# Opening with four heads' keys in float32 by k and a fixed order; block products with B22 in buffers of its own and T3 by accumulating transfers

## The chip, the cores and the metric

The kernel runs on one core of one Trainium2 chip. The metric is the device time of one execution in microseconds; the median of several runs counts. Engines are named as in the profile: PE is TensorE (matrix products, with PEld its weight loads), DVE is VectorE, ACT is ScalarE, POOL is GpSimd and SP is the sync engine, which here only issues transfers.

## The reference, cut to what matters

One decoder layer over x (512 tokens, 1024 channels) with a memory mem (256 rows of 1024). h = RMSNorm(x) is projected into five branches (a convolution module, stick-breaking attention, an mLSTM, a gated linear recurrence, attention over the memory); each branch is gated, projected up to 1024 channels, weighted with a sigmoid gate and summed. The sum goes through one output projection, x is added, and a last RMSNorm follows. All inputs and outputs are float32.

```python
y_m = memory_attention(m_q, rmsnorm(mem, mem_norm_g), w_mkv) * silu(m_z)   # keys and values: mem_n @ w_mkv
...
for n, y in enumerate((y_a, y_b, y_c, y_d, y_m)):
    merged = merged + gates[:, :, n] * (y @ w_up[n])
x = x + merged @ w_out
return rmsnorm(x, final_norm_g)
```

## The kernel before, in words

**Numbers.** Nearly every float32 product is made of three single-pass products: each operand is split into a rounded high part (`hi`, one copy on ACT) and a rest (`lo`, one subtraction on DVE), and hi*hi + hi*lo + lo*hi are accumulated. Products of plain float32 operands are also possible; each of them shows as two records in the trace. A second way to make `lo` is used where DVE is the busier engine: ACT writes -f, rounded, into lo, and a transfer issued from POOL adds f to it in place (`accum_op=ALU.add`).

**Program order and queues.** The program is written with a planner that orders the instructions of each engine by a simulated timeline and puts in the semaphores. Instructions of one engine run in the order that the planner gave them, and so do the transfers of one issuing engine. `tc.high_priority` moves instructions forward in that plan, `tc.issue_after(ins)` keeps what is inside behind `ins` on the same engine, and `behind(ends)` does so for several. Pools have a fixed number of buffers under each tag; a tile waits until a buffer of its tag is released.

**Weights.** `load_w` (line 161) brings a 512 KB block into one of two staging buffers (`wst`) through SP's queue and splits it in two halves into the tags `whi` and `wlo` (six buffers each). The staging buffer comes free when both halves are split, and only then can the next block but one be issued. `queued` holds the last such transfer.

**Opening** (lines 250 to 375). Ten small products warm TensorE up. Then come:

- the memory's keys, `keys(h)`: for heads 0 and 1 float32 products of the weights `wkf[h]` with the scaled, transposed memory `mt` (8 steps of 128 channels, `k`); for heads 2 and 3 split operands (`memH`, `memL`, and weights through `load_w`), head after head;
- the memory's values, `values(u, w)`: four blocks of two k each, 12 products of 512 columns a block (two row halves, three products, two k);
- x: four tiles of 128 tokens are loaded, squared and summed on ACT, scaled on DVE by the root of the mean (`rx`, line 342), transposed on TensorE (`x_T(k)`, four 128x128 transposes for one of three `pj` banks), and evicted into `hH` (ACT) and `hL` (DVE);
- the row sums of mem, two transposes of their roots (`rps`), and the scaling of keys and values.

The order in which TensorE takes the values and the transposes is left to the planner.

**Middle.** `STEPS` and `ENDS` list, by hand, the order of projections, heads, gates (`G`) and up-projections (`U`).

**End** (lines 1100 to 1300). The output projection is done as seven block products over a 2x2 division (512-row halves of the weights by 512-column halves), from sums and differences of blocks. The weights' blocks and their combinations are called b11, b21, n4, T1, T2, T3 and b22; `operand` (line 1077) splits such a block into `woH` and `woL` (six buffers of each). `product` issues the products for two row tiles into two PSUM banks (`X`, `Z`, `W`, `Y`, `L`), `take` adds a bank to the residual rows `xr` on DVE, and `finish` squares a finished piece on ACT (`junk`, with the sum in `ss`), collects the sums (`v`), prepares `quarter`, multiplies the row with the norm's weights (line 1207), and for the last piece of a row tile takes the root (`root`, ACT), forms 1/root with one Newton step (DVE), scales both halves and issues the two stores. Some banks are used twice without clearing: the second product into X, the one with T3, may begin only when `take` has read what the first left there, and likewise the last product, with b22, on Y.

T3's blocks load through `block` into the staging tag `wst`, are subtracted in place (`minus`), and are split with ACT and DVE. b22 loads into the same two staging buffers, after them, and is split with accumulating transfers. `s2_end` and `s4_end` are the last splits of two sums of the left operand.

Of the kernel before, what the change touches and what calls it, by code (L numbers as in the profile page):

```python
# [80 lines left out]
def build(ctx, tc, x, mem, memT, cols_d, rows_d, wcm, wbv, wcv0, wcv1, wmk, wmv, wup, wout, dw, fg, out):  # L81
# [78 lines left out]

    def load_w(src, n, scale=None, stage=wpool):

        st = stage.tile([P, 1056], F32, tag="wst", name="wst", bufs=WST)
        queued[0] = nc.sync.dma_start(out=st[:, :n], in_=src)
        res = []
        m = n // 2
        for half in range(2):
            hi = wpool.tile([P, 576], F32R, tag="whi", name="whi", bufs=WHL)
            lo = wpool.tile([P, 576], F32R, tag="wlo", name="wlo", bufs=WHL)
            f = st[:, half * m:(half + 1) * m]  # L170
            with tc.high_priority(offset=PREP):
                if scale is None:
                    act(hi[:, :m], f, AF.Copy)  # L173
                    V.tensor_tensor(out=lo[:, :m], in0=f, in1=f32(hi[:, :m]), op=ALU.subtract)  # L174
# [85 lines left out]
    wkf = [spool.tile([P, D], F32, name=f"wkf{h}") for h in range(2)]  # L260
# [30 lines left out]
    def keys(h, w=None):  # L291

        ps = kps[h // 2][:, (h % 2) * NMEM:(h % 2 + 1) * NMEM]
        for k in range(NK):
            go, end = h % 2 == 0 and k == 0, k == NK - 1
            if w is None:
                mm(ps, lhsT=wkf[h][:, k * P:(k + 1) * P], rhs=mt[:, k, :], start=go, stop=end, skip_group_check=True)  # L297
            else:
                mm3(ps, [(*piece(w, k, P, 4), memH[:, k, :], memL[:, k, :])], first=go, last=end, check=True)

    keys(0)
    keys(1)
# [4 lines left out]
    wk = [load_w(wmk[h], D, stage=spool) for h in (2, 3)]  # L307
    keys(2, wk[0])
    keys(3, wk[1])
# [8 lines left out]
    def values(u, w):  # L318
        for kk in range(2):
            k = 2 * u + kk  # L320
            wh, wl = piece(w, kk, 512, 1)
            for m in range(2):
                sl = slice(m * P, (m + 1) * P)
                mm(vps[m], lhsT=memH[:, k, sl], rhs=wh, start=k == 0, stop=False)
                mm(vps[m], lhsT=memH[:, k, sl], rhs=wl, start=False, stop=False)
                mm(vps[m], lhsT=memL[:, k, sl], rhs=wh, start=False, stop=k == NK - 1)

    def x_T(k):
        tp = pj.tile([P, S], F32, tag="pj", name="tp")
        for i in range(NT):  # L330
            nc.tensor.transpose(tp[:, i * P:(i + 1) * P], xt[i][:, k * P:(k + 1) * P], ident)
        act(hH[:, k, :], tp, AF.Copy, scale=col("norm_g", k))
        V.scalar_tensor_tensor(out=hL[:, k, :], in0=tp, scalar=col("norm_g", k), in1=f32(hH[:, k, :]),
                               op0=ALU.mult, op1=ALU.subtract)

    values(0, wv[0])
    values(1, wv[1])
# [5 lines left out]
    for k in range(4):  # L343
        x_T(k)
    values(2, load_w(wmv[2], D))
    for k in range(4, NK):
        x_T(k)
    values(3, load_w(wmv[3], D))
# [7 lines left out]
    for m in range(2):  # L356
        nc.tensor.transpose(rps[:, m * P:(m + 1) * P], rc[:, m:m + 1].broadcast_to([P, P]), ident)
# [719 lines left out]
    def operand(f, add=False):  # L1077
# [3 lines left out]
        if add:  # L1081
            act(lo, f, AF.Copy, scale=-1.0)
            G.dma_start(out=lo, in_=f, accum_op=ALU.add)
            act(hi, f, AF.Copy)
        else:
            split_sb(f, hi, lo)
# [96 lines left out]
    def finish(t, half, cs=slice(0, S)):  # L1183
# [15 lines left out]
        if end:  # L1199
            V.tensor_scalar(v, ss, sums[t], 0.25, op0=ALU.add, op1=ALU.mult)  # L1200
        else:
            V.tensor_scalar_add(v, ss, sums.get(t, EPS))
        sums[t] = v
        if n == pieces[t] - 1:
            quarter[t] = epool.tile([P, 1], F32, name=f"quarter{t}")
            V.tensor_scalar_mul(quarter[t], v, 0.25)
        V.tensor_tensor(out=xo, in0=xo, in1=rows[:, cs], op=ALU.mult)
        if not end:
            return
# [34 lines left out]
    with behind(s4_end):  # L1244
        b22 = [operand(block(1, 1, u), True) for u in range(2)]
# [20 lines left out]
def _layout(a):  # L1266
# [25 lines left out]
    wmk = wm[:, :, :E].reshape(NK, P, 4, P).transpose(2, 1, 0, 3).reshape(4, P, NK * P)  # L1292
# [30 lines left out]
```

## Time and profile before

| | us |
|---|---|
| median of 3 runs | 840.95 (840.57 to 841.35) |
| the profiled execution | 839.85 |
| its span | 838.1 |
| PE busy | 821.7 |
| DVE, ACT busy | 599.2, 499.4 |
| DMA, mean | 131 GB/s |

The profile is of one execution. Its span runs from the first to the last recorded instruction; 1.75 us of its time lie around the span. A row of the timeline gives the start, the duration from there to the end of the last of its instructions, engine, line, operation, out<-in, shape and count, and in square brackets how long the engine had been idle before it and what ended that wait. Rows with a count of several are merged neighbours. Matmuls overlap, so the distance between starts is the cost of one, not the duration in its row.

### The profile page before, as it was taken

How to read it: one execution, taken by the hardware profiler on the slowest of the kernel's cores; microseconds unless marked ns; L12 is line 12 of the kernel's file. 1: busy time of each engine (PE TensorE's matmuls, PEld its weight loads, DVE VectorE, ACT ScalarE, POOL GpSimd, SP SyncE). 2: the span in 40 equal slices, each digit the busy share in tenths (PEclk: the TensorE clock that was granted, in tenths of full speed). 3: DMA queues.
4: the chain of work that ended last, by engine and by line, in shares of the span. 5: the costliest groups of instructions: out<-in, count | busy, mean ns of one | idle time of the engine just before them, and what ended most of it. 6: DMA issues, size and time to landing. Idle time of an engine off the chain costs nothing.

```text
span 838.1 us, 11376 instructions
## 1 busy us (share of the span) xinstructions
PE 821.7 (98%) x4028; PEld 693.8 (83%) x4028; DVE 599.2 (71%) x1139; ACT 499.4 (60%) x895; POOL 105.2 (13%) x157
## 2 busy tenths in 40 slices
PE   8999999999999999999999999999999999999995
PEld 7788888888898889788888988888888888888874
DVE  4879989997456677785675767559667575458976
ACT  6644475635545554667556546585465977954564
POOL 0000020101100222022333000010100200200020
PEclk9999999999999999999999999999999999999998
DMA  9432274445624334436625243563352745675184
GB/s 356 155 128 98 89 152 112 105 123 134 156 88 126 90 88 101 119 88 144 152 77 121 80 142 98 145 157 101 108 132 75 154 119 147 138 254 195 37 212 128
DMA packets 36848, 109.47 MB, mean 131 GB/s; under 512 B 4148, under 2 KB 4276, under 8 KB 36792
## 3 DMA queue, kind: packets, MB, share of 16 engines
q1 hardware_dynamic: 24376, 84.11, 30.7%
q0 software_dynamic: 11552, 23.07, 16.3%
q10 hardware_dynamic: 864, 1.57, 0.5%
q8 instruction: 31, 0.51, 0.2%
q14 instruction: 25, 0.20, 0.1%
HBM read 103.49 MB, written 2.11 MB: 126 GB/s over the span
## 4 chain that ended last, share of the span: by engine, by line
PE 89%; DVE 6%; DMA 2%; ACT 2%; issue 1%; ACTq 0%; SPq 0%; DVEq 0%
PE pj L212 24%; PE pj L211 24%; PE pj L210 24%; PE pj L541 2%; PE pj L539 2%; PE pj L540 2%; PE po L653 1%; PE wb L639 1%; DMA wst<-in 1%; PE og L844 1%; PE mk L297 1%; DVE wlo L174 1%; PE zb L610 1%; PE zb L609 1%; DMA mt<-in 1%; DVE woL L229 1%
## 5 line engine op out<-in xcount | busy, mean ns | idle before, releaser
L212 PE MATMUL pj<-hH,wlo 128*128 128x512 f32 x768 | 300.0, 391 | 0.3 <-DVE wlo L174 0.3
L211 PE MATMUL pj<-hL,whi 128*128 128x512 f32 x768 | 299.7, 390 | 0.0
L210 PE MATMUL pj<-hH,whi 128*128 128x512 f32 x768 | 299.5, 390 | 0.0
L173 ACT ACTIVATE whi<-wst 128x512 fp32r<-128x512 f32 (+1 forms) x180 | 111.6, 630 | 161.6 <-PE pj L211 116.9
L174 DVE TENSOR_TENSOR wlo<-wst,whi 128x512 fp32r<-128x512 f32 (+1 forms) x180 | 122.2, 686 | 75.5 <-ACT whi L173 75.1
L212 PEld LDWEIGHTS pj<-hH,wlo 128*128 128x128 f32 x768 | 144.2, 188 | 30.3 <-DVE wlo L174 0.7
L211 PEld LDWEIGHTS pj<-hL,whi 128*128 128x128 f32 x768 | 144.3, 188 | 29.7
L210 PEld LDWEIGHTS pj<-hH,whi 128*128 128x128 f32 x768 | 144.3, 188 | 29.2
L194 POOL DMA_DIRECT2D wlo<-in x72 | 62.7, 871 | 531.8 <-ACT wlo L193 394.8
L427 DVE SCALAR_TENSOR_TENSOR acc<-u,cols,acc 128x512 f32<-128x512 f32 x120 | 88.6, 746 | 1.4
L195 ACT ACTIVATE whi<-wst 128x512 fp32r<-128x512 f32 x72 | 45.3, 630 | 55.6 <-PE pj L211 40.0
L211 PE MATMUL pj<-yL,whi 128*128 128x512 f32 x160 | 62.5, 390 | 0.0
L210 PE MATMUL pj<-yH,whi 128*128 128x512 f32 x160 | 62.4, 391 | 0.0
L212 PE MATMUL pj<-yH,wlo 128*128 128x512 f32 x160 | 62.3, 390 | 0.0
L193 ACT ACTIVATE wlo<-wst 128x512 fp32r<-128x512 f32 x72 | 44.5, 618 | 5.9 <-PE at L540 4.0
L212 PEld LDWEIGHTS pj<-yH,wlo 128*128 128x128 f32 x160 | 30.0, 188 | 6.2
L210 PEld LDWEIGHTS pj<-yH,whi 128*128 128x128 f32 x160 | 30.0, 188 | 6.1
L211 PEld LDWEIGHTS pj<-yL,whi 128*128 128x128 f32 x160 | 30.1, 188 | 5.9
L629 DVE TENSOR_TENSOR_SCAN kp<-kp 128x512 f32<-128x512 f32 (+3 forms) x32 | 26.8, 858 | 10.9 <-POOL kp L622 10.6
L540 PE MATMUL pj<-wlo,hH 128*128 128x256 f32 (+1 forms) x112 | 31.8, 284 | 0.0
L541 PE MATMUL pj<-whi,hL 128*128 128x256 f32 (+1 forms) x112 | 31.8, 284 | 0.0
L539 PE MATMUL pj<-whi,hH 128*128 128x256 f32 (+1 forms) x112 | 31.5, 283 | 0.0
(395 smaller groups left out, 1262.3 us busy)
## 6 DMA issues: line engine op xcount, KB each, us to landing
wst<-in SPq DMA_DIRECT2D x132, 512.0 KB, 3.3
wlo<-in POOLq DMA_DIRECT2D x72, 256.0 KB, 5.2
xt<-in SPq DMA_DIRECT2D x4, 512.0 KB, 9.4
raw<-in SPq DMA_DIRECT2D x4, 512.0 KB, 6.6
t<-in SPq DMA_DIRECT2D x4, 512.0 KB, 5.2
woL<-t POOLq DMA_DIRECT2D x4, 512.0 KB, 6.4
wst<-in SPq DMA_DIRECT2D x2, 528.0 KB, 4.3
mr<-in SPq DMA_DIRECT2D x2, 512.0 KB, 10.6
```

The costliest lines, as they stand in the source:

```text
L173: act(hi[:, :m], f, AF.Copy)
L174: V.tensor_tensor(out=lo[:, :m], in0=f, in1=f32(hi[:, :m]), op=ALU.subtract)
L193: act(lo[:, :m], st[:, sl], AF.Copy, scale=-1.0)
L194: G.dma_start(out=lo[:, :m], in_=src[:, sl], accum_op=ALU.add)
L195: act(hi[:, :m], st[:, sl], AF.Copy)
L210: mm(ps, lhsT=ah, rhs=bh, start=first and i == 0, stop=False, skip_group_check=check)
L211: mm(ps, lhsT=ah, rhs=bl, start=False, stop=False, skip_group_check=check)
L212: end = mm(ps, lhsT=al, rhs=bh, start=False, stop=last and i == n - 1, skip_group_check=check)
L427: V.scalar_tensor_tensor(out=a, in0=u[:, k:k + S], scalar=col("a_w", i * 31 + k), in1=a, op0=ALU.mult, op1=ALU.add)
L539: mm(dst[t], lhsT=hH[:, k, tsl], rhs=wh, start=first, stop=False, skip_group_check=True)
L540: mm(dst[t], lhsT=hH[:, k, tsl], rhs=wl, start=False, stop=False, skip_group_check=True)
L541: mm(dst[t], lhsT=hL[:, k, tsl], rhs=wh, start=False, stop=k == NK - 1, skip_group_check=True)
```

## The change

In the opening all four heads' keys are float32 products. Their weights come in a layout by k (`wkf`, 128 x 8 x 512), in pieces of one, one, two, two and two k, over ACT's queue (the first three) and SP's, with mt in four pieces of one, one, two and four k. The products run k by k with the heads inside; no key weight is split any more. TensorE's order of values, transposes and the two `rps` transposes is written out (`in_order`), and each eviction of a transpose is queued behind the last value split so far (`prep`), so that the third and the fourth value block are split earlier than the planner put them.

At the end, the T3 blocks are split with accumulating transfers, and b22 is loaded in four halves into four `wlo` buffers right after the last projections' weights, ahead of T3's loads in SP's queue, and split by halves from there. The table of functions that holds the root is loaded behind the last s4 split. In `finish`, the row multiplication of a piece that is not the last comes behind `v` and `quarter`.

```diff
-    wkf = [spool.tile([P, D], F32, name=f"wkf{h}") for h in range(2)]
+    wkf = spool.tile([P, NK, 4 * P], F32, name="wkf")
...
-    for i in range(2):
-        sl = slice(i * 512, i * 512 + 512)
-        nc.scalar.dma_start(out=wkf[0][:, sl], in_=wmk[0][:, sl])
-    nc.scalar.preload_act_table_set("sqrt_and_others")
-    for c in ((0, 2), (2, 4), (4, 8)):
-        nc.sync.dma_start(out=mt[:, c[0]:c[1], :], in_=memT[:, c[0]:c[1], :])
-    nc.sync.dma_start(out=wkf[1], in_=wmk[1])
+    for i, c in enumerate((slice(0, 1), slice(1, 2), slice(2, 4), slice(4, 8))):
+        nc.sync.dma_start(out=mt[:, c, :], in_=memT[:, c, :])
+        if i < 3:
+            nc.scalar.dma_start(out=wkf[:, c, :], in_=wmk[:, c, :])
+        if i == 1:
+            nc.scalar.preload_act_table_set("sqrt_and_others")
+    for c in (slice(4, 6), slice(6, 8)):
+        nc.sync.dma_start(out=wkf[:, c, :], in_=wmk[:, c, :])
...
-    keys(0)
-    keys(1)
+    for k in range(NK):
+        for h in range(4):
+            end = mm(kps[h // 2][:, (h % 2) * NMEM:(h % 2 + 1) * NMEM], lhsT=wkf[:, k, h * P:(h + 1) * P],
+                     rhs=mt[:, k, :], start=h % 2 == 0 and k == 0, stop=k == NK - 1, skip_group_check=True)
...
-    wk = [load_w(wmk[h], D, stage=spool) for h in (2, 3)]
-    keys(2, wk[0])
-    keys(3, wk[1])
...
+    last_pe = [end]
+    def in_order(f):
+        with tc.issue_after(last_pe[0].ins):
+            last_pe[0] = f()
...
+        with behind(prep):
+            act(hH[:, k, :], tp, AF.Copy, scale=col("norm_g", k))
+            V.scalar_tensor_tensor(out=hL[:, k, :], in0=tp, scalar=col("norm_g", k), in1=f32(hH[:, k, :]),
+                                   op0=ALU.mult, op1=ALU.subtract)
...
+    wv.append(load_w(wmv[2], D))
+    prep = prepared[0]
+    for u, kk in ((0, 0), (0, 1), (1, 0)):
+        values(u, kk, wv[u])
...
+    values(1, 1, wv[1])
+    x_T(0)
+    x_T(1)
+    values(2, 0, wv[2])
+    wv.append(load_w(wmv[3], D))
+    prep = prepared[0]
+    x_T(2)
+    x_T(3)
+    values(2, 1, wv[2])
+    x_T(4)
+    x_T(5)
+    values(3, 0, wv[3])
+    x_T(6)
+    x_T(7)
+    values(3, 1, wv[3])
...
         if add:
-            act(lo, f, AF.Copy, scale=-1.0)
-            G.dma_start(out=lo, in_=f, accum_op=ALU.add)
-            act(hi, f, AF.Copy)
+            parts = f if isinstance(f, list) else [f]
+            w = D // len(parts)
+            for i, p in enumerate(parts):
+                sl = slice(i * w, (i + 1) * w)
+                act(lo[:, sl], p, AF.Copy, scale=-1.0)
+                G.dma_start(out=lo[:, sl], in_=p, accum_op=ALU.add)
+            for i, p in enumerate(parts):
+                act(hi[:, i * w:(i + 1) * w], p, AF.Copy)
...
+    b22_raw = []
+    for u in range(2):
+        halves = []
+        for c in range(2):
+            f = f32(wpool.tile([P, 576], F32R, tag="wlo", name="wlo", bufs=WHL))[:, :S]
+            with tc.issue_after(queued[0].ins):
+                queued[0] = nc.sync.dma_start(out=f, in_=wout[1, 2 + u, :, c * S:(c + 1) * S])
+            halves.append(f)
+        b22_raw.append(halves)
...
         if end:
             V.tensor_scalar(v, ss, sums[t], 0.25, op0=ALU.add, op1=ALU.mult)
+            V.tensor_tensor(out=xo, in0=xo, in1=rows[:, cs], op=ALU.mult)
         else:
-            V.tensor_scalar_add(v, ss, sums.get(t, EPS))
+            prior = V.tensor_scalar_add(v, ss, sums.get(t, EPS))
...
-            V.tensor_scalar_mul(quarter[t], v, 0.25)
-        V.tensor_tensor(out=xo, in0=xo, in1=rows[:, cs], op=ALU.mult)
+            prior = V.tensor_scalar_mul(quarter[t], v, 0.25)
         if not end:
+            with behind((prior,)):
+                V.tensor_tensor(out=xo, in0=xo, in1=rows[:, cs], op=ALU.mult)
             return
...
-            T3.append(operand(minus(f, t2[u], f)))
+            T3.append(operand(minus(f, t2[u], f), True))
...
     with behind(s4_end):
-        b22 = [operand(block(1, 1, u), True) for u in range(2)]
+        nc.scalar.preload_act_table_set("sqrt_and_others")
+        b22 = [operand(f, True) for f in b22_raw]
```

More of the change, by code (lines that the diff above doesn't have):

```diff
@@ L159, in build @@
     t1, t2, n4 = [], [], []
+    prepared = [None]
     def load_w(src, n, scale=None, stage=wpool):
@@ L172, in load_w @@
                 if scale is None:
-                    act(hi[:, :m], f, AF.Copy)
-                    V.tensor_tensor(out=lo[:, :m], in0=f, in1=f32(hi[:, :m]), op=ALU.subtract)
+                    prepared[0] = (act(hi[:, :m], f, AF.Copy),
+                                   V.tensor_tensor(out=lo[:, :m], in0=f, in1=f32(hi[:, :m]), op=ALU.subtract))
                 else:
@@ L289, in build @@
     vps = [at.tile([P, S], F32, tag="at", name="mv") for _ in range(2)]
[L291 to L299, printed above, removed]
-    keys(0)
-    keys(1)
+    for k in range(NK):
+        for h in range(4):
+            end = mm(kps[h // 2][:, (h % 2) * NMEM:(h % 2 + 1) * NMEM], lhsT=wkf[:, k, h * P:(h + 1) * P],
+                     rhs=mt[:, k, :], start=h % 2 == 0 and k == 0, stop=k == NK - 1, skip_group_check=True)
     for c in range(4):
@@ L316, in build, with values, go @@
     mr = [load_row(mem, i, "mr") for i in range(2)]
[L318 to L321, printed above, removed]
+    last_pe = [end]
+    def in_order(f):
+        with tc.issue_after(last_pe[0].ins):
+            last_pe[0] = f()
+    def values(u, kk, w):
+        k = 2 * u + kk
+        wh, wl = piece(w, kk, 512, 1)
+        def go():
             for m in range(2):
@@ L325, in values, with go @@
                 mm(vps[m], lhsT=memH[:, k, sl], rhs=wl, start=False, stop=False)
-                mm(vps[m], lhsT=memL[:, k, sl], rhs=wh, start=False, stop=k == NK - 1)
+                end = mm(vps[m], lhsT=memL[:, k, sl], rhs=wh, start=False, stop=k == NK - 1)
+            return end
+        in_order(go)
     def x_T(k):
         tp = pj.tile([P, S], F32, tag="pj", name="tp")
[L330 to L337, printed above, removed]
+        def go():
+            for i in range(NT):
+                end = nc.tensor.transpose(tp[:, i * P:(i + 1) * P], xt[i][:, k * P:(k + 1) * P], ident)
+            return end
+        in_order(go)
+        with behind(prep):
[6 more added lines that the diff above has]
+        values(u, kk, wv[u])
     for i, t in enumerate(xt):
@@ L342, in build @@
         V.tensor_scalar_mul(t, t, rx[:, i:i + 1])
[L343 to L348, printed above, removed]
+    values(1, 1, wv[1])
[13 more added lines that the diff above has]
+    values(3, 1, wv[3])
     nc.sync.dma_start(out=rows, in_=rows_d.broadcast_to([P, NROW]))
@@ L356, in build @@
     for m in range(2):
-        nc.tensor.transpose(rps[:, m * P:(m + 1) * P], rc[:, m:m + 1].broadcast_to([P, P]), ident)
+        in_order(lambda: nc.tensor.transpose(rps[:, m * P:(m + 1) * P], rc[:, m:m + 1].broadcast_to([P, P]), ident))
     rm = spool.tile([P, NMEM], F32, name="rm")
@@ L1291, in _layout @@
     wm = a["w_mkv"][0].reshape(NK, P, 2 * E)
-    wmk = wm[:, :, :E].reshape(NK, P, 4, P).transpose(2, 1, 0, 3).reshape(4, P, NK * P)
+    wmk = wm[:, :, :E].transpose(1, 0, 2)
     wmv = wm[:, :, E:].reshape(4, 2, P, E).transpose(0, 2, 1, 3).reshape(4, P, 2 * E)
```

## The prediction

> **What bounds the kernel now.** I read the page first, then the busy times by stretch, then the timeline of the opening and of the end, engine by engine, and last the rows of the accumulating transfers.
>
> ```profile
> span 838.1 us, 11376 instructions
> PE 821.7 (98%) x4028; PEld 693.8 (83%) x4028; DVE 599.2 (71%) x1139; ACT 499.4 (60%) x895; POOL 105.2 (13%) x157
> ```
>
> TensorE idles 838.1 - 821.7 = 16.4 us in all. The rows below place about 12 of these at the two ends, so a change there can only win by fewer or denser products in the opening, by shorter waits in the last products, or by a shorter stretch after the last product. The middle has nothing to give. The opening:
>
> ```profile
> 6.57:14.90 8.33, 7.35 (x32) 5.78 (x33) 5.51 (x11) 6.80 (x13) 0.00 (x0) 1.00 1.03 419
> 20.85:26.32 5.47, 5.47 (x27) 4.46 (x26) 4.59 (x12) 2.74 (x6) 0.00 (x0) 1.00 0.78 304
> ...
> 1.43 4.64 PE L252 MATMUL warm<-ident 128*128 128x128 f32 x20 [1.43 <-POOL ident masks.py:199]
> 6.57 1.13 PE L297 MATMUL mk<-mt,wkf 128*128 128x256 f32 x4 [0.51 <-DVE mt L285]
> 8.49 1.13 PE L297 MATMUL mk<-mt,wkf 128*128 128x256 f32 x4 [0.78 <-DVE mt L285]
> 9.81 5.45 PE L297 MATMUL mk<-mt,wkf 128*128 128x256 f32 x24 [0.19 <-ACT mt L287]
> 14.90 0.47 PE L210 MATMUL mk<-memH,whi 128*128 128x256 f32 x1
> ...
> 26.32 1.47 PE L331 MATMUL tp<-ident,xt 128*128 128x128 f32 x12
> ...
> 29.13 1.32 PE L331 MATMUL tp<-ident,xt 128*128 128x128 f32 x8 [1.13 <-DVE hL L333]
> ...
> 37.00 0.47 PE L210 MATMUL pj<-hH,whi 128*128 128x512 f32 x1
> ...
> 37.96 0.50 PE L212 MATMUL pj<-hH,wlo 128*128 128x512 f32 x1 [0.25 <-DVE wlo L174]
> ```
>
> The two window rows give length, busy time of PE, PEld, DVE, ACT and POOL, clock, DMA share and GB/s. The keys start at 6.57, half a microsecond after the warm-up products, wait 0.78 and 0.19 for scaled pieces of mt, and end at 20.85 where the values begin. The projections start at 37.00 and stumble once (0.25 for wlo). Clock 1.00 throughout.
>
> **The keys.** Heads 0 and 1 are 16 float32 products that show as 32 records; the run of 24 lasts from 9.81 to 14.90, 0.212 us each, so 0.424 a product. Heads 2 and 3 are 48 single-pass products from 14.90 to 20.85, 0.124 each, 0.372 for three. Turning them into float32 adds 16 x (0.424 - 0.372) = 0.8 us of TensorE: alone, a loss. Against it stands the order by k. A k needs 128 KB of mt and 256 KB of weights for 4 x 0.424 = 1.7 us of products, 0.23 MB per us, while the window row shows 419 GB/s arriving, so past the first two pieces TensorE should not starve.
>
> ```profile
> 6.17 0.61 DVE L285 TENSOR_SCALAR mt<-mt,cols 128x256 f32<-128x256 f32 x2 [1.76 <-DMA mt<-in]
> ...
> 11.90 2.17 ACT L173 ACTIVATE whi<-wst 128x512 fp32r<-128x512 f32 x4
> ...
> 12.72 2.49 DVE L174 TENSOR_TENSOR wlo<-wst,whi 128x512 fp32r<-128x512 f32 x4
> ...
> 21.98 2.73 DVE L342 TENSOR_SCALAR xt<-xt,rsq_t 128x1024 f32<-128x1024 f32 x4
> ...
> 29.33 1.16 ACT L173 ACTIVATE whi<-wst 128x512 fp32r<-128x512 f32 x2
> ...
> 31.62 2.85 SPq L164 DMA_DIRECT2D wst<-in  x2
> ```
>
> The first mt piece (256 KB) is there at 6.17; half the size should be there earlier, but the warm-up holds TensorE to 1.43 + 4.64 = 6.07. I take a start at 6.1 and 32 x 0.424 = 13.6 us: the keys end at 19.7 instead of 20.85. The four whi and four wlo splits of the third and fourth head (2.17 on ACT, 2.49 on DVE) go; both engines wait for data around there, so I count nothing for that. The bytes ahead of x are the same, so x arrives as before.
>
> **The fixed order.** From 20.85 on TensorE has 48 value products at 5.47 / 24 = 0.228 (10.9 us) and 34 transposes at 1.47 / 12 = 0.12 (4.1). After: 6.1 + 13.6 + 10.9 + 4.1 = 34.7, against 37.00 plus some 0.6 for the first products (three took 37.00 to 38.29 where two steps later it is 0.23 each): effectively 37.6. A dense opening is worth 2.9. What was late before is the split of the third value block, at 29.33, although ACT was busy for only 2.74 of the 5.47 us before 26.32; it holds a staging buffer, so the weights of the first projections were issued only around 31.62. The order now queues the evictions of the transposes behind that split, which pulls the issue forward by some 4 us, and the projections can start on time. What can be late next: x is scaled by 21.98 + 2.73 = 24.7 at the earliest; the four value steps ahead of the first transpose end at 19.7 + 4 x 6 x 0.228 = 25.2. The margin is 0.5, and new splits compete for DVE there. I take 0.5 of stall: -2.4. Ends: -2.9, and +0.8 if the dearer keys buy nothing.
>
> **The end.** Times are those of the profile before.
>
> ```profile
> 798.99 2.35 DVE L1090 TENSOR_TENSOR wst<-t,wst 128x1024 f32<-128x1024 f32 x2
> ...
> 809.12 0.67 DVE L1179 TENSOR_TENSOR xr0L<-xr0L,pj 128x512 f32<-128x512 f32 x1
> ...
> 818.74 0.15 DVE L1202 TENSOR_SCALAR v<-ss 128x1 f32<-128x1 f32 x1 [4.44 <-ACT junk L1193]
> ...
> L229 DVE TENSOR_TENSOR woL<-wst,woH x2: 1208/1210/1212, 805.5 to 806.7; 128x1024 fp32r<-128x1024 f32 x2
> ...
> 800.30 2.20 ACT L229 ACTIVATE woH<-wst 128x1024 fp32r<-128x1024 f32 x2
> ...
> 816.09 1.06 ACT L1082 ACTIVATE woL<-wst 128x1024 fp32r<-128x1024 f32 x1 [2.03 <-DMA wst<-in]
> ...
> 809.94 0.47 PE L210 MATMUL pj<-woH,s2H 128*128 128x512 f32 x1 [1.79 <-DVE xr0L L1179]
> ...
> 822.56 0.47 PE L210 MATMUL pj<-woH,s4H 128*128 128x512 f32 x1 [1.18 <-DVE merged L1179]
> ...
> 828.73 0.28 PE L212 MATMUL at<-woH,s4L 128*128 128x128 f32 x1
> ```
>
> *T3 by accumulating transfers.* Before the T3 product TensorE waits 1.79 us for the eviction of X, which DVE issues at 809.12 behind the two splits woL<-wst, 2 x 1.21 = 2.4 us. They leave DVE, so the eviction comes near 806.7, before the 809.94 - 1.79 = 808.15 at which TensorE wants the bank: the wait goes. In their place come two ACT copies, two transfers on POOL's queue, and their landing. T3's blocks are formed by 798.99 + 2.35 = 801.3, the first half of that by 800.2; ACT is free at 800.30, so the two POOL issues are near 801.4 and 803.4, and T1's two and B22's four queue behind them.
>
> ```profile
> L1083 POOL DMA_DIRECT2D woL<-t x2: 867/869/871, 793.6 to 795.2; - x2
> DMA to landing us min/median/max: 6.0/6.4/6.8
> ...
> DMA to landing us min/median/max: 4.5/4.8/9.3
> ...
> 791.40:796.90 5.50, 5.50 (x26) 4.51 (x24) 5.43 (x12) 5.50 (x9) 1.74 (x2) 1.00 0.38 72
> 796.90:802.40 5.50, 5.50 (x25) 4.51 (x24) 5.50 (x11) 4.86 (x10) 2.20 (x4) 1.00 0.95 216
> ```
>
> The first landing row is T2's pair, issued at 793.6 and 795.2, so landed at about 799.6 and 802.0, 2.4 apart; the second is T1's and B22's four. With 4.5 to 6.4 the first half of T3 lands at 806 to 808, the second, 2.4 later, at 808.5 to 810; they are wanted at about 808.2 and 809.6 (six products on). I take 0.3 of new wait: -1.5. Ends: -1.8, and with 9.3 for the second (812.7, 3.1 late) +1.3.
>
> By the Trainium skill (SBUF — State Buffer, the section on two separate sides) a transfer issued from POOL can be starved of its descriptors while DVE holds the port pair they share; by that rule each of the eight issues could come one DVE operation, some 0.6 us, late, and the sum would be lighter by about 0.6. Here the two POOL issues beside a DVE that was busy 5.43 of 5.50 us took 0.87 each, as the later ones did, so this trace does not bear it out.
>
> *B22 in buffers of its own.* Before, B22 loads into the staging buffers of T3, and ACT waits for it 2.03 us ahead of 816.09, with the squares of the third row block queued behind. DVE waits 4.44 us for those squares until 818.74, and the eviction of Y behind that costs TensorE 1.18 at 822.56. In the change the four half loads take low-half weight buffers as the last projections free them, ahead of the output products, and T3's own loads queue behind them on SP: these blocks are not used until 798.99, so that costs nothing. ACT no longer waits: -1.2, ends -1.2 and 0. POOL's four issues of half the size cost 4 x 0.87 where nobody waits for POOL. Without the two stalls B22 is wanted 3 us sooner, at 819.6 and 821.0; eight transfers 2.4 apart per 512 KB from 806.6 bring its last quarter at 806.6 + 5 x 2.4 = 818.6. It fits by two microseconds.
>
> *After the last product.*
>
> ```profile
> 823.25 1.28 ACT L1196 ACT_TABLE_LOAD   x1
> 824.54 0.29 ACT L1196 ACTIVATE root<-ss,quarter 128x1 f32<-128x1 f32 x1
> ...
> 832.28 0.15 DVE L1206 TENSOR_SCALAR quarter<-v 128x1 f32<-128x1 f32 x1
> ...
> 832.74 0.29 ACT L1196 ACTIVATE root<-ss,quarter 128x1 f32<-128x1 f32 x1 [0.44 <-DVE quarter L1206]
> ...
> 834.47 0.34 ACTq L1219 DMA_DIRECT2D out<-xr1L  x1
> ```
>
> The last product ends at 829.0, the last result leaves at 834.47. In between DVE works off a backlog that began at 823.25, where a table load holds the first root and DVE waits behind it. The load moves to about 800, where ACT pays the same 1.28; quarter, held until 832.28 by the row multiplication, comes directly behind v. Undelayed, the way is eviction 0.3, square 0.5, root 0.3, reciprocals 0.6, scaling 0.7, with 0.2 of handovers 2.6, against 834.47 - 829.01 = 5.5: 2.8 at best. Finishing four row blocks keeps DVE occupied, so I take -2.0; ends -2.8 and 0.
>
> The Trainium skill (ScalarE: Activation LUTs, what a table load costs) puts a switch at some 2.7 us with its drain; by that, moving it would be worth 1.4 more, and the sum 8.5. In the trace the root starts at 824.54, 0.01 after the load ends, so 1.28 is the price here.
>
> **Sum.** -2.4 - 1.5 - 1.2 - 2.0 = -7.1. The profiled execution took 839.85 us (838.1 and 1.75 around it), so 832.75; the median of the runs, 840.95, lies 1.1 above it: 833.8. From no change a measurement tells about 0.2%, 1.7 us.
>
> **Rivals.**
> - *The opening gives little.* The order is rigid: if scaling of x or a value split comes 2 us late, TensorE waits where it used to choose another product. For: margin 0.5 at 25.2. Against: DVE has 2.5 us less to do. Then -0.3 instead of -2.4: 835.9.
> - *The end gives little.* T3 lands 3.1 late and B22 follows: T3 +1.3, Y and end -1.5 together, opening -2.4: 838.3. For: the 9.3 row; DMA share 0.95 between 796.9 and 802.4. Against: that 9.3 lay beside B22's plain loads, which move away.
> - *Slower.* The accumulating transfers run one behind the other at s per 512 KB. B22's last quarter lands at 806.6 + 5s and is wanted at 821.0, so it delays above s = 2.9 and eats the whole sum at s = (7.1 + 14.4) / 5 = 4.3. At 4.5, the shortest single landing, it is 8.1 late: 842. Against: T2's pair landed 2.4 apart.
> - *No effect.* The planner reorders the middle and new waits there give the gain back: 840. TensorE has no idle there that shows such sensitivity.
>
> **How the numbers follow.** Forecast 0.62, opening 0.16, end 0.10, slower 0.05, no effect 0.07. The forecast's own range, from its ends, is 831 to 835.6; taking in the first two rivals gives 830.8 to 838.3, with some 0.15 outside. Faster 0.87, same 0.07, slower 0.06.
>
> **What would show it.** Right: first key product near 6.1, 64 float32 key records without a gap, first projection product by 35.2, at most 0.5 of wait at the T3 product and none at the last, no table load after the last product's start, last output issued within 4 us of the last product. Wrong: waits of products on hL, wlo or xt before 35; TensorE waiting for woL in T3 or B22; DVE idle on ACT near the evictions; idle TensorE between 40 and 780.

## The result, and the profile after

The changed kernel takes 834.44 us in the median of four runs (834.15 to 834.65), the kernel before 840.76 in four (839.69 to 841.35): a ratio of 0.9929 (95% interval 0.9917 to 0.9941). The forecast was 833.8 with a range of 830.8 to 838.3. The profiled execution of the changed kernel took 834.15 us with a span of 832.1; before it was 839.85 and 838.1. So the span lost 6.0 us, where the prediction had summed 7.1. The head of the page:

```profile
span 832.1 us, 11361 instructions
PE 821.4 (99%) x4012; PEld 694.0 (83%) x4012; DVE 595.1 (72%) x1133; ACT 499.5 (60%) x897; POOL 108.8 (13%) x161
```

TensorE is as busy as before (821.4 against 821.7), so nearly all of the gain is idle time: 832.1 - 821.4 = 10.7 us instead of 16.4. The opening in the timeline of TensorE, then two rows of DVE and one of ACT (the split of the third value block, which was at 29.33 before):

```profile
5.51 1.99 PE L296 MATMUL mk<-mt,wkf 128*128 128x256 f32 x8
8.97 12.35 PE L296 MATMUL mk<-mt,wkf 128*128 128x256 f32 x56 [1.47 <-DVE mt L288]
20.97 0.81 PE L325 MATMUL mv<-whi,memH 128*128 128x512 f32 x2
...
36.19 0.48 PE L212 MATMUL pj<-hH,whi 128*128 128x512 f32 x1
...
784.52 0.39 PE L212 MATMUL pj<-woH,aH 128*128 128x512 f32 x1
...
8.56 0.35 DVE L288 TENSOR_SCALAR mt<-mt,cols 128x256 f32<-128x256 f32 x1 [3.11 <-DMA mt<-in]
...
23.21 2.73 DVE L354 TENSOR_SCALAR xt<-xt,rsq_t 128x1024 f32<-128x1024 f32 x4
...
26.16 1.14 ACT L175 ACTIVATE whi<-wst 128x512 fp32r<-128x512 f32 x2
```

The keys start earlier (5.51 against 6.57) but wait 1.47 us for the second piece of mt, which DVE could scale only at 8.56, and they end no earlier: the values begin at 20.97 against 20.85. From there TensorE runs without a gap to the first projection product at 36.19. The first product of the output projection comes at 784.52 instead of 785.91. That is what the opening brought: 1.4 us. The distance between these two points was 748.9 and is 748.3; before, it held the stumble of 0.25 for wlo at 37.96, and now there is no wait in it. The three places of TensorE before that the end is compared with:

```profile
785.91 0.39 PE L210 MATMUL pj<-woH,aH 128*128 128x512 f32 x1
...
809.94 0.47 PE L210 MATMUL pj<-woH,s2H 128*128 128x512 f32 x1 [1.79 <-DVE xr0L L1179]
...
822.56 0.47 PE L210 MATMUL pj<-woH,s4H 128*128 128x512 f32 x1 [1.18 <-DVE merged L1179]
```

The end now, in the timelines of TensorE, ACT and POOL:

```profile
809.15 0.50 PE L213 MATMUL pj<-woL,s2H 128*128 128x512 f32 x1 [0.74 <-DMA woL<-wst]
...
824.88 0.28 PE L214 MATMUL at<-woH,s4L 128*128 128x128 f32 x1
...
799.27 1.28 ACT L1283 ACT_TABLE_LOAD   x1
800.56 1.06 ACT L1107 ACTIVATE woL<-wst 128x1024 fp32r<-128x1024 f32 x1
...
808.77 1.13 ACT L1107 ACTIVATE woL<-wlo 128x512 fp32r<-128x512 f32 x2
...
828.24 0.34 ACTq L1257 DMA_DIRECT2D out<-xr1L  x1
...
801.92 0.89 POOL L1108 DMA_DIRECT2D woL<-wst  x1 [2.40 <-ACT woL L1107]
803.82 0.87 POOL L1108 DMA_DIRECT2D woL<-wst  x1 [1.00 <-ACT woL L1107]
```

The stall of 1.79 at the start of the T3 product is gone, and so is the 1.18 at the last product. In their place TensorE waits 0.74 in the middle of the T3 product for the second half of T3's low part (its gap in the sequence of products is 0.91). ACT no longer waits for b22: its copies run from 808.77 without an idle time. The last product ends at 825.16, and 6.94 us are left to the end of the span, where 9.09 were left before.

| part | before | after | gain | predicted |
|---|---|---|---|---|
| first output product | 785.91 | 784.52 | 1.4 | 2.4 |
| gap at T3 | 1.94 | 0.91 | 1.0 | 1.5 |
| gap at the last product | 1.35 | 0 | 1.35 | 1.2 |
| end of last product to end | 9.09 | 6.94 | 2.15 | 2.0 |

Together 5.9 of the 6.0 us. A gap is the distance between the starts of two products less the 0.23 us that a product takes there.

### The profile page after: what moved, and what is told of

The parts are those of the page before. It is cut to its first block, busy times and chain, and to the rows that moved or that the text cites. A ratio compares the mean times of both kernels' runs of the same rounds, so it can differ in the third digit from the quotient of the medians.

```text
span 832.1 us, 11361 instructions
## 1 busy us (share of the span) xinstructions
PE 821.4 (99%) x4012; PEld 694.0 (83%) x4012; DVE 595.1 (72%) x1133; ACT 499.5 (60%) x897; POOL 108.8 (13%) x161
## 4 chain that ended last, share of the span: by engine, by line
PE 90%; DVE 4%; DMA 4%; ACT 1%; issue 1%; POOL 0%; SPq 0%; POOLq 0%; ACTq 0%
PE pj L213 25%; PE pj L214 25%; PE pj L212 25%; PE pj L562 2%; PE pj L560 2%; PE pj L561 2%; DMA xt<-in 1%; PE po L674 1%; PE wb L660 1%; DMA mt<-in 1%; DVE wlo L176 1%; PE og L865 1%; DMA woL<-wst 1%; PE zb L631 1%; PE zb L630 1%
## 5 line engine op out<-in xcount | busy, mean ns | idle before, releaser
L175 ACT ACTIVATE whi<-wst 128x512 fp32r<-128x512 f32 (+1 forms) x176 | 109.4, 630 | 159.9 <-PE pj L213 117.5
L176 DVE TENSOR_TENSOR wlo<-wst,whi 128x512 fp32r<-128x512 f32 (+1 forms) x176 | 119.9, 687 | 76.6 <-ACT whi L175 76.1
```

The costliest lines, as they stand in the source:

```text
L175: prepared[0] = (act(hi[:, :m], f, AF.Copy), V.tensor_tensor(out=lo[:, :m], in0=f, in1=f32(hi[:, :m]), op=ALU.subtract))
```

## The experiments

Some kernels were executed only once; they have one time and one profile. The same kernel scatters by one to three microseconds (the kernel before took 839.12 to 842.22 in thirteen executions), so for those the places in the profile are compared rather than the times.

**The opening alone, with the end as it was before.**

```diff
-            T3.append(operand(minus(f, t2[u], f), True))
+            T3.append(operand(minus(f, t2[u], f)))
...
-        nc.scalar.preload_act_table_set("sqrt_and_others")
-        b22 = [operand(f, True) for f in b22_raw]
+        b22 = [operand(block(1, 1, u), True) for u in range(2)]
...
```

> The opening of the changed kernel with the end of the kernel before. If the two parts add up: the projections start near 36.2 as in the changed kernel, the first output product comes 1.4 us earlier than before, and everything after it is as before (waits of 1.8 and 1.2 us on the evictions, 9.1 us after the last product), so the span is 836.7 and the time 1.4 below before. If the opening's gain is used up by the old end, which DVE's queue and not TensorE sets there, the span stays within 0.5 of 838.1.

Measured: 839.35 us against 839.92, ratio 0.999 (0.9981 to 0.9999). The profile is of the fastest of ten executions, 837.97 with a span of 836.3; the median of the ten spans is 837.65. In TensorE's timeline:

```profile
5.85 14.59 PE L295 MATMUL mk<-mt,wkf 128*128 128x256 f32 x64
20.09 0.81 PE L324 MATMUL mv<-whi,memH 128*128 128x512 f32 x2
...
27.08 0.73 PE L324 MATMUL mv<-whi,memH 128*128 128x512 f32 x2 [0.28 <-ACT whi L174]
...
36.28 0.48 PE L211 MATMUL pj<-hH,whi 128*128 128x512 f32 x1
...
808.05 0.48 PE L211 MATMUL pj<-woH,s2H 128*128 128x512 f32 x1 [1.20 <-DVE xr0L L1199]
```

In this execution the pieces of mt came in time. All 64 key records run without a gap and the values begin at 20.09, 0.9 us earlier than in the changed kernel, but the projections begin at 36.28, no earlier. TensorE waits for the third value block's split instead (0.28 at 27.08). The stall at the T3 product (1.20, at 808.05) is back, and the one at the last product too (1.18). So the profiled execution agrees with the first theory, but the median of the spans lies within 0.5 of 838.1, as the second has it: beside the old end most executions show little of the opening's gain. Which wait took it there can't be said, since only this one trace was kept.

**The end alone, with the opening as it was before.**

```diff
-    for k in range(NK):
-        for h in range(4):
...
+    keys(0)
+    keys(1)
...
-        in_order(go)
```

> The opening of before with the end of the changed kernel. If the parts add up: span 833.5, time 4.6 below before, with the wait of 0.7 for the second half of T3, none before the last product, and 6.9 us after it. If the end only gains because the opening moved work, less than 3.5 below before.

Measured: 836.5 against 839.92, ratio 0.9958 (0.9943 to 0.9973), span 834.2.

```profile
786.45 0.39 PE L212 MATMUL pj<-woH,aH 128*128 128x512 f32 x1
811.13 0.51 PE L213 MATMUL pj<-woL,s2H 128*128 128x512 f32 x1 [0.80 <-DMA woL<-wst]
```

From the first output product to the end it takes 47.75 us (47.58 in the changed kernel, 52.19 before), so the end's gain does not need the new opening. The spans of the profiled executions add up: 838.1 - 836.3 = 1.8 for the opening, 838.1 - 834.2 = 3.9 for the end, 5.7 of 6.0. The medians don't: 0.6 and 3.4, so 4.0 where the whole change gained 6.3. Counted from the end alone to the whole change, the ratio goes from 0.9958 to 0.9929, which gives the opening 2.4 us. Its 1.4 us fit both intervals, but that the two parts are independent is not shown.

**The fixed order with the keys of before.**

```diff
-    for k in range(NK):
-        for h in range(4):
-            end = mm(kps[h // 2][...], lhsT=wkf[:, k, h * P:(h + 1) * P], rhs=mt[:, k, :], ...)
...
+    keys(0)
+    keys(1)
...
+    wk = [load_w(wmk[h], D, stage=spool) for h in (2, 3)]
+    keys(2, wk[0])
+    end = keys(3, wk[1])
```

> The changed kernel with the keys of before (two heads in float32, two split, head by head), and the written-out order of values and transposes kept. Theory A: the opening's gain comes from the written-out order alone, since the keys end at 20.97 against 20.85 before; then the projections start near 36.1 and the time is that of the changed kernel within 0.4. Theory B: it comes from the keys in float32, which take eight splits off ACT and DVE; then the projections start near 37.5 and the time is 1.3 above the changed kernel.

Measured: 834.27 against 839.92, ratio 0.9938 (0.9914 to 0.9962), span 832.3; the changed kernel's own ratio is 0.9929 (0.9917 to 0.9941).

```profile
20.98 0.40 PE L335 MATMUL mv<-whi,memH 128*128 128x512 f32 x1
...
36.15 0.48 PE L212 MATMUL pj<-hH,whi 128*128 128x512 f32 x1
...
26.10 1.15 ACT L175 ACTIVATE whi<-wst 128x512 fp32r<-128x512 f32 x2 [0.91 <-DMA wst<-in]
```

With the old keys the values begin at 20.98 and the projections at 36.15. All that the opening brought is the written-out order, together with the evictions queued behind the splits (these two were not tried apart); the float32 keys by k bring nothing that can be seen.

**Fewer key products.** Of the 32 key products 12 are left out (heads 2 and 3, all k but the first and last), so the keys are incomplete and TensorE has less to do ahead of the values.

```diff
         for h in range(4):
+            if h > 1 and 0 < k < NK - 1:
+                continue
```

> The changed kernel with 12 of the 32 key products left out (heads 2 and 3 keep k 0 and 7 only), 5.1 us less work for TensorE in the opening. Theory A: the opening is set by what arrives (the third value block is split only when it lands, near 26): the projections start at 36.2 within 0.3 and the span is 832.1 within 0.4. Theory B: TensorE's work sets it, as in the forecast's sum: the projections start near 31.5 to 33 and the span is 827.5 to 829.

Measured: 836.03 in one execution, span 834.0. In TensorE's timeline:

```profile
18.54 0.73 PE L327 MATMUL mv<-whi,memH 128*128 128x512 f32 x2 [1.12 <-ACT whi L175]
...
36.70 0.48 PE L212 MATMUL pj<-hH,whi 128*128 128x512 f32 x1
```

Taking 12 x 2 x 0.21 = 5 us of work off TensorE does not bring the projections forward at all: it waits 2.4 for pieces of mt between the keys, 1.12 for the first value block's split, 0.79 for the second's and 0.33 for x. The opening is set by arrivals and by what ACT and DVE do with them. The span is 1.9 above the changed kernel's, where the first theory allowed 0.4: the projections start 0.5 later, and 1.2 more is lost between them and the first output product, 0.9 of it in one wait of TensorE for a gate.

**The scaled memory in pieces of two k.**

```diff
-    for i, c in enumerate((slice(0, 1), slice(1, 2), slice(2, 4), slice(4, 8))):
+    for c in (slice(0, 2), slice(2, 4), slice(4, 8)):
         nc.sync.dma_start(out=mt[:, c, :], in_=memT[:, c, :])
...
```

> The changed kernel with the scaled memory in pieces of two, two and four k (the cut of the kernel before), so that the second k no longer waits for a piece of its own; all else as changed. Theory A (by now: the opening is set by the landing of the third value block, not by when the keys end): the gap of 1.47 us in the keys goes, the values start near 20.3 instead of 20.97, but the first projection product stays at 36.1 to 36.4, because ACT splits the third block near 26.2 as before and TensorE waits for it some 0.3 to 0.6 us; span 832 within half a microsecond. Theory B (TensorE's own work sets it, and the late piece of mt cost the change its gain): the first projection product comes 0.6 us sooner, 35.6, and the span is near 831.5.

Measured: 834.6 in one execution, span 832.6.

```profile
20.23 0.81 PE L325 MATMUL mv<-whi,memH 128*128 128x512 f32 x2
...
36.04 0.48 PE L212 MATMUL pj<-hH,whi 128*128 128x512 f32 x1
```

The gap in the keys goes and the values begin 0.74 us earlier; 0.15 of it is left at the projections. The late piece of mt, which looks like the loss in the changed kernel's trace, is not what the change lost.

**T3 split on DVE again.**

```diff
-            T3.append(operand(minus(f, t2[u], f), True))
+            T3.append(operand(minus(f, t2[u], f)))
```

> The changed kernel with T3 split by ACT and DVE again. If DVE's queue set the eviction of X: the two splits (2.4 us) stand ahead of it again and TensorE waits 1.2 to 1.9 us at the first T3 product instead of 1.0 us inside it; span 832.4 to 833.0. If the wait before came only from ACT standing at B22's load, it does not come back: span 831.2.

Measured: 836.91 in one execution (the kernel before beside it: 841.56), span 835.2. TensorE's wait, and the second of the two splits and the eviction on DVE:

```profile
810.60 0.47 PE L212 MATMUL pj<-woH,s2H 128*128 128x512 f32 x1 [2.25 <-DVE xr0L L1215]
...
807.98 1.21 DVE L231 TENSOR_TENSOR woL<-wst,woH 128x1024 fp32r<-128x1024 f32 x1
...
809.78 0.68 DVE L1215 TENSOR_TENSOR xr0L<-xr0L,pj 128x512 f32<-128x512 f32 x1
```

The eviction stands behind the two splits again and TensorE waits 2.25, somewhat more than the first theory had. From the first output product to the end it takes 49.09, 1.5 more than in the changed kernel. The rest of the longer span lies ahead of the end: 0.4 in the opening and 1.2 between it and the first output product, 0.9 of that in the same wait for a gate as in the run with fewer keys, which does not have this edit.

**The table load moved to where ACT has room,** behind the last sigmoid of the gates.

```diff
+    with tc.issue_after(last_gate[0].ins):
+        nc.scalar.preload_act_table_set("sqrt_and_others")
...
     with behind(s4_end):
-        nc.scalar.preload_act_table_set("sqrt_and_others")
```

> The changed kernel with the load of the root's table behind the last gate, where ACT has been idle for over 2 us, instead of behind the last s4 split. Theory A: the second half of T3 lands late because the table load (1.28 us) stands ahead of T3's copies on ACT; then both POOL issues come 1.3 us earlier, the wait of 0.74 in the T3 product goes, span 831.2 to 831.4. Theory B: the transfers on POOL's queue are bound by the rate of the DMA engines and land when they do; the wait stays above 0.5, span 831.9 or more.

Measured: 833.43 in one execution, span 831.4.

```profile
798.95 1.06 ACT L1108 ACTIVATE woL<-wst 128x1024 fp32r<-128x1024 f32 x1
...
800.31 0.89 POOL L1109 DMA_DIRECT2D woL<-wst  x1 [1.10 <-ACT woL L1108]
```

T3's transfers are issued 1.6 us earlier and no product at the end waits. First output product to end: 46.65, 0.93 less than in the changed kernel, which is the 0.91 of the T3 gap.

**The finish as before, without the early table load.**

```diff
-            prior = V.tensor_scalar_mul(quarter[t], v, 0.25)
+            V.tensor_scalar_mul(quarter[t], v, 0.25)
+        V.tensor_tensor(out=xo, in0=xo, in1=rows[:, cs], op=ALU.mult)
...
-        nc.scalar.preload_act_table_set("sqrt_and_others")
```

> The changed kernel with the old order in finish (row multiplication ahead of v and quarter) and without the early load of the root's table. Theory A (the two edits to the finish are worth what the stretch after the last product became shorter, 9.09 to 6.94): the table load, 1.28 us, stands between v and the first root after the last product started, the stretch from the end of the last product to the end is 8.5 to 9.1 us instead of 6.94; T3's first copy moves 1.3 us up on ACT as the table load is gone from there, so the wait of 0.91 in the T3 product goes; span near 833.2. Theory B (the stretch became shorter because DVE was not late any more, after the stall at b22 had gone, and the finish order hardly matters): the stretch stays at 7.0 to 7.5, and the span is near 831.5.

Measured: 833.9 in one execution, span 831.9. The table load on ACT and TensorE's last product:

```profile
816.75 1.28 ACT L1232 ACT_TABLE_LOAD   x1
...
823.88 0.28 PE L214 MATMUL at<-woH,s4L 128*128 128x128 f32 x1
```

The last product ends at 824.16, with no wait in T3, and 831.9 - 824.16 = 7.74 us follow. That is between the two theories, nearer to the second: of the 2.15 us by which this stretch had become shorter, 0.80 hang on the two edits to the finish and 1.35 come without them. And the two edits as they stand in the change win nothing: the table load costs 0.91 at T3 and the finish gives 0.80 back. Only with the load moved, as in the run above, do they pay.

**b22 through the staging buffers, after T3.**

```diff
-    b22_raw = []
...
-        b22 = [operand(f, True) for f in b22_raw]
+        b22 = [operand(block(1, 1, u), True) for u in range(2)]
```

> The changed kernel with B22 through the two staging buffers, as before. If the buffers of its own are what freed the last product: the load waits until T3's transfers have read the staging buffers (near 809), ACT stands at it, and TensorE waits 1.2 us or more before the last product; span 833.3 to 835. If T3's move off DVE was enough, no wait there and span 832.1.

Measured: 839.69 in one execution, span 837.8. Waits of TensorE, one of ACT, and a window row:

```profile
809.92 0.50 PE L213 MATMUL pj<-woL,s2H 128*128 128x512 f32 x1 [1.06 <-DMA woL<-wst]
815.18 0.50 PE L213 MATMUL pj<-woL,s4H 128*128 128x512 f32 x1 [0.80 <-DMA woL<-t]
...
819.00 0.63 PE L213 MATMUL pj<-woL,s4H 128*128 128x512 f32 x1 [2.15 <-DMA woL<-t]
...
819.25 1.06 ACT L1107 ACTIVATE woL<-wst 128x1024 fp32r<-128x1024 f32 x1 [4.30 <-DMA wst<-in]
...
819.00:822.40 3.40, 3.40 (x8) 2.63 (x9) 0.47 (x3) 2.62 (x4) 0.86 (x1) 0.53 0.41 80
```

First output product to end: 837.8 - 784.98 = 52.8 us, 5.2 more than in the changed kernel and more than before (52.2). So the first theory had the loss right, but not its place: no product waits for b22. b22's second block is split at 819.25, where before it was split at 816.09, since T3's transfers hold the staging buffers until they have landed. Yet the products that wait are those with T1 (`woL<-t`). T1's two accumulating transfers were issued at 806.33 and 808.68 and waited for until 815.18 and 819.00, 8.8 and 10.3 us, with b22's plain loads running beside them; in the changed kernel no accumulating transfer took more than 8.0. After the longer wait the granted clock was 0.53 for 3.4 us (the third number from the end of the window row), and eight products took 0.43 us each instead of 0.23. The two gaps (1.0 and 2.3), the slow products (1.5) and 0.3 more at T3 make up 5.1 of the 5.2 us. So what b22's own buffers do beside T3's accumulating split is more than the 1.2 at the last product: they take b22's plain loads out of this stretch. That it is the plain loads which made T1's transfers late is the likeliest reading of one execution; no run moves the loads alone.

**A candidate with three changes:** the table load moved as above, mt in pieces of two k, and the third and fourth value block loaded early into a part of `merged` that is unused by then.

```diff
+    early = [merged[:, 2 * u:2 * u + 2, :].rearrange("p a b -> p (a b)") for u in (1, 2)]
+    for u, t in zip((2, 3), early):
+        nc.sync.dma_start(out=t, in_=wmv[u])
...
```

> A candidate that changes three things in the changed kernel: (1) the table load behind the last gate (worth 0.93 us at the end where it was tried alone), (2) the third and fourth value block loaded into a part of merged that is still unused, right behind the second block and ahead of the memory rows and of rows, so that they need not wait for a staging buffer, (3) the scaled memory in pieces of two, two and four k. Theory A (the third block's landing sets the opening): ACT splits the third block before 24, no wait in values or transposes, and the first projection product comes when TensorE's own work is done: keys from 6.0, 14.2 us of keys, 15.2 us of values and transposes, so 35.4 to 35.6 instead of 36.19; together with 0.93 at the end the span is near 830.5 and the time 1.6 us below the changed kernel's, ratio to it 0.998. Theory B (the scaling of x or the evictions on DVE are just as late): waits of TensorE on x or on hL appear in place of those for the value blocks, the first projection stays at 36.0 to 36.3, and only the 0.93 at the end is won: span near 831.2. Theory C (1 MB more ahead of the memory rows delays their root, which the last transposes of the opening need): TensorE waits there, 36.5 or later.

The changed kernel beside it:

> The changed kernel unaltered, to stand beside the candidate on the same chip: 834.4, span 832.1 to 832.6, ratio to the kernel before 0.993. The place of the first projection product tells how far the landing of single pieces varies: 36.1 to 36.4 by theory A.

Measured: the candidate 833.29 (832.87 to 834.97, five runs), ratio to the kernel before 0.992 (0.9907 to 0.9933); the changed kernel 833.95 (833.85 to 835.2, five runs), 0.9927 (0.9913 to 0.9941). The spans of the profiled executions are 831.2 and 831.8. The candidate's median is 0.7 us lower, which these runs don't tell from no difference. TensorE and ACT of the candidate:

```profile
34.27 0.66 PE L341 MATMUL tp<-ident,xt 128*128 128x128 f32 x4 [0.91 <-DVE hL L347]
36.29 0.48 PE L213 MATMUL pj<-hH,whi 128*128 128x512 f32 x1
...
21.44 1.14 ACT L176 ACTIVATE whi<-merged 128x512 fp32r<-128x512 f32 x2
```

ACT splits the third block at 21.44 instead of 26, and TensorE does not wait for it any more, but it waits 0.91 at the last transposes for the evictions hL, and the projections start at 36.29. In the second profile of the changed kernel, where the projections start at 36.33, that wait is there too, 0.39. So the landing of the third block, to which I had by then ascribed the opening, is not its only limit; a second one lies directly behind. The gain expected from the opening did not come, as the second theory had it.

**The candidate with less work on DVE.**

```diff
-        V.tensor_scalar_mul(t, t, rx[:, i:i + 1])
+        V.tensor_scalar_mul(t[:, :8], t[:, :8], rx[:, i:i + 1])
```

> The candidate with three changes, but the scaling of the four x tiles on DVE covers only the first 8 of their 1024 columns; the rest of the scaling is left out (2.73 us of DVE work become some 0.4), all else equal. It asks what held the opening of the candidate at 36.29 although its third and fourth value blocks were split from 21.44 and 23.48 on. Theory A (DVE's own work between the scaling and the evictions hL is the second limit, directly behind the landing of the third block): with 2.3 us less on DVE the wait of 0.91 us on hL goes, TensorE runs without a gap from the end of the keys near 20.6 and the first projection product comes 15.2 us later, at 35.7 to 35.9; the span is 0.5 us below the candidate's 831.2, near 830.7. Theory B (the evictions wait for something else, ACT's copies hH or the buffers of the transposes): the wait stays and the first projection product stays at 36.2 to 36.4.

Measured: 833.1 in one execution, span 831.0. TensorE, then ACT, then DVE:

```profile
34.30 0.66 PE L341 MATMUL tp<-ident,xt 128*128 128x128 f32 x4 [0.91 <-DVE hL L347]
36.32 0.48 PE L213 MATMUL pj<-hH,whi 128*128 128x512 f32 x1
...
28.92 0.69 ACT L346 ACTIVATE hH<-tp,cols 128x512 fp32r<-128x512 f32 x1 [0.45 <-PE tp L341]
...
27.25 0.17 DVE L274 TENSOR_SCALAR rc<-rc 128x2 f32<-128x2 f32 x1 [1.01 <-ACT merged L271]
...
30.38 0.68 DVE L177 TENSOR_TENSOR wlo<-wst,whi 128x512 fp32r<-128x512 f32 x1
...
32.30 1.28 DVE L177 TENSOR_TENSOR wlo<-wst,whi 128x512 fp32r<-128x512 f32 x2
33.51 2.06 DVE L347 SCALAR_TENSOR_TENSOR hL<-tp,cols,hH 128x512 fp32r<-128x512 f32 x3
```

The wait is the same 0.91. Relieved of 2.1 us, DVE idled 1.0 just before 27.25 and was no earlier with the evictions. So the scaling of x is not what holds them. Ahead of the first copy hH ACT squares the memory rows, but that delay is over by 28.92, where ACT waits 0.45 for TensorE's next transposes. What is left in the rows are four splits of the first projections' weights (2.6 us), which stand among the evictions on DVE between 30.38 and 33.5; the eviction that ends the wait starts right behind the last two. That these splits hold the last transposes is read from the rows; no run moved them.

## Why the prediction was right, and where its steps were off

The time lay 0.6 us from the forecast, and the four places were the ones that moved. The closeness is partly luck: the profiled execution missed the forecast for it by 834.15 - 832.75 = 1.4, and the median of the changed kernel lay only 0.3 above its profiled execution, not 1.1.

*The keys, and the opening's sum.* This is the step that failed. "I take a start at 6.1 and 32 x 0.424 = 13.6 us: the keys end at 19.7" and from that 34.7 + 0.5 for the opening. The start was early enough, at 5.51; the end came at 20.97, because of a wait of 1.47 that I had not priced: my argument from the rate spoke of what comes "past the first two pieces", and the wait is at the second, which was late at 8.56. (Without a gap the 64 records took 20.09 - 5.85 = 14.2 us in the run with the opening alone and 20.32 - 6.59 = 13.7 in the candidate.) But the deeper error is that the sum counts TensorE's work alone. With the keys ending at 20.1, at 20.2 or at 21.0, or with 5 us of them left out, the projections began between 36.0 and 36.7. In the changed kernel's own profile TensorE runs dense from 8.97 to 36.19, so there its work and the other limits happen to end together; whenever the keys ended earlier, a wait took their place. For everything beside TensorE the sum had 0.5, from the margin for x; the split of the third block, which waits for its landing near 26.1 to 26.4, and the evictions hL each allow no more than about 36. The 2.9 us of a dense opening were there only down to that, 1.4. The order was the right mechanism, shown by the run that has it with the old keys; the bound was mis-sized. Two smaller steps were off as well. "So x arrives as before" did not hold: x was scaled by 23.21 + 2.73 = 25.94 instead of 24.71, though with most of this scaling left out the projections came no earlier. And the order pulled the next weights' issue from 31.62 to 28.28, by 3.3 us and not "some 4".

*T3.* Moving the splits off DVE was the right mechanism: with them back, the end takes 1.5 us more. The term was 1.5 and came to 1.0. The new wait was put at 0.3 and measured as a gap of 0.91 (of that 0.74 in the row; the row has 0.29 to 0.86 in other runs with the same end). The step that failed is "ACT is free at 800.30, so the two POOL issues are near 801.4 and 803.4". In the changed kernel's clock, 1.4 us earlier, that would be 800.0 and 802.0; the issues are at 801.92 and 803.82. In another paragraph I had moved the table load to "about 800, where ACT pays the same 1.28", and I did not carry it into the queue ahead of T3's first copy. Moving the load away brought the first issue to 800.31 and removed the wait, so this is shown, in one execution. The landing itself was within the rows: issued at 803.82, waited for until 809.15, 5.3 us.

*B22.* -1.2 predicted, 1.35 measured, and no product waited for b22. What the prediction missed is that the edit is a condition of the other: with b22 in the staging buffers T1's transfers were waited for until 10.3 us after their issue. In a rival I had noted that the 9.3 of the kernel before lay beside b22's plain loads, but gave their moving away no term of its own.

*After the last product.* The size was right (2.0 and 2.15), the reason only in part: I gave it all to the table load and to quarter. With both edits undone the stretch was 7.74, so 0.80 of the gain came from the edits and 1.35 without them. The likely reason of the 1.35 is that DVE had no stalled row block to catch up with once the wait at b22 had gone; no run shows that by itself, since with b22 in the staging buffers TensorE came later too and the stretch stayed at 6.8. The last result is issued 3.1 us after the last product (825.16 to 828.24), within the 4 that I gave.

*The rivals.* The opening gave little, but not so little that its rival (-0.3) was the case; beside the old end, where the median gained 0.6, it was near. T3 landed 0.9 late and not 3.1; accumulating transfers one after the other did not happen, since b22's copies and products did not wait; the middle did not react in the changed kernel's profiles. One reading of the prediction was off without harm: the idle times in its rows and after the last product add up to 16.3 of the 16.4 us, not to about 12.

*The two rules that were weighed.* By the Trainium skill (SBUF — State Buffer, on two separate sides) POOL's issues could be starved beside a busy DVE. The issue at 801.92 took 0.89 beside a DVE that was busy 5.50 of 5.50 us, as the window row shows (the third busy time): again not seen. But this was no test of the rule, since DVE ran a TENSOR_TENSOR at that time, and the same section of the Trainium skill reports that such instructions did not hold transfers up; so the 0.6 that I worked out by it was not to be expected here.

```profile
796.90:802.40 5.50, 5.50 (x25) 4.49 (x24) 5.50 (x11) 5.32 (x7) 2.68 (x5) 1.00 0.96 267
```

By the Trainium skill (ScalarE: Activation LUTs, on what a table load costs) the switch would cost some 2.7 us; the rows here show 1.28 at 799.27, with the next copy at 800.56, and 1.28 with the old finish at 816.75; T3 lost 0.91 to it.

## What to carry to other kernels

When a stage becomes dense by a better order, its new length need not be the sum of the bound engine's work; it is the latest of all the arrivals and side engines that the old order hid; list each one's own earliest end, and take the latest. An instruction that is moved off one critical spot (here a table load of 1.28 us) has to be put into the queue where it lands and added to everything behind it there: 0.91 of it came back, until it was placed where nobody waited. Two edits that meet in one place (accumulating transfers, and plain loads that run beside them and share their buffers) must be priced together; one without the other lost 5 us here. And a profile is of one execution: where its time lies well below the median, as with the opening alone, its gain is not to be added to another's.

## What the runs showed of the hardware that was not expected

- A single early load lands at quite different times in executions of one kernel. In the first profile of the changed kernel TensorE waited 1.47 us for the second piece of mt; in the second profile of the same kernel the 64 key records ran without a gap and the values began at 20.23 instead of 20.97. The first projection product was at 36.19 and 36.33 all the same.
- After the wait of 2.15 us in the run with b22 through the staging buffers the granted clock was 0.53 from 819.0 to 822.4, and a product took 0.43 us instead of 0.23. The kernel before kept a clock of 1.00 after its wait of 1.79. What makes the difference no run shows.
- Accumulating transfers within SBUF took 4.4 to 8.0 us to land in the changed kernel, and up to 10.3 with b22's plain loads among them. These are the landing times of the tile woL, first of the changed kernel, then of the run with b22 through the staging buffers (minimum, median, maximum):

```profile
DMA to landing us min/median/max: 4.4/6.3/8.0
```

```profile
DMA to landing us min/median/max: 4.4/6.2/10.3
```
